# The opening of a hybrid attention layer: who loads the identity, the first norm's weights and x's first columns, and who casts the first weights

## The chip, the cores and the metric

The kernel runs on one core of one Trainium2 chip. The metric is the device time of one execution in microseconds (us); lower is better. A time given as a median is that of several runs; times inside an execution come from one profiled execution, counted from the start of its span.

## The reference, cut to what matters

One layer over 256 tokens of 2048 features, in float32. The change touches only how the layer begins: the first RMSNorm and the first columns of the first projection.

```python
def rms_norm(x, g):
    y = x32 * lax.rsqrt(jnp.mean(x32 * x32, axis=-1, keepdims=True) + EPS)
    return (y * g).astype(x.dtype)

h = rms_norm(x, attn_norm[layer])          # x is (1, 256, 2048)
proj = h @ w_in_l                          # (2048, 6152): q, k, v of two head groups, 8 forget gates
...                                        # forgetting attention and stick-breaking attention
x = x + merged @ w_out_l
x = x + conv_ffn(rms_norm(x, ffn_norm))    # two further products, a depthwise convolution of width 3
```

## The kernel before, in words

Tokens lie in 128 partitions, as two tiles `xt[0]` and `xt[1]` of 128 tokens (`x2`, line 82). For the projection x is needed with features in partitions, so TensorE (PE) transposes it: a 128x128 block of x times an identity matrix. `transposed_split(k, g)` (line 130) does this for the two blocks of columns k and k+1: four transposes into one PSUM tile `ps_x`, then two ScalarE (ACT) instructions that multiply by the norm's weight of each feature (`g`, one number for each partition) and round to fp32r, the high part of `hT` (line 140), then two VectorE (DVE) instructions that compute what the rounding left, the low part (line 143). The factor 1/rms of each token is applied later to the product's rows.

Weights are handled in the same way: a piece lands in a raw tile, one instruction casts it to fp32r (`w_hi`) and a DVE subtraction gives `w_lo`. Each product is three matmuls: high times high, low part of hT times high, high times low.

The norm's weights reach the kernel as 16 rows of 128 (`prow[:KT]`). `columns(ga, ...)` (line 123) turns them into 16 columns: one PE transpose with the identity (line 125) and one DVE copy (line 126). So the identity (`cs[:, :P]`, 64 KB of the constants) and `prow` come ahead of the first transposed x.

`opening()` (line 353) computes the first 512 columns of the projection in 8 chunks of 256 features. Its loads, casts and products are written out in order by hand: inside the block at line 429 a manual schedule keeps PE, DVE, ACT and SyncE (SP) in the order of the program, so an instruction that waits holds up all that stands behind it on its engine. GpSimd (POOL) is not in that list, and has no other work in the opening than to fill the tile `zeros`.

- `load_x(k, n)` (line 86) loads n blocks of columns of both token tiles, always by SP.
- `load_w(c, queue, which)` (line 359) loads chunk c of the weights, 256 rows of 512 columns. Chunk 0 is loaded as two halves of 128 rows, 256 KB each; below, the first half and the second half.
- `split_w(c)` (line 368) casts and subtracts. For the first half of chunk 0 it calls `transposed_split(0, ga)` between the cast and the subtraction (line 376).
- `multiply(c, i, n, high)` (line 381) issues the matmuls on a piece, first those with `w_hi`, then those with `w_lo`.
- `keep_busy(n)` (line 347) issues n matmuls of zeros whose result nobody reads, so that PE does not stand still. They need the tile `zeros` (line 343), which POOL fills.

The order of the issues and of the first work is lines 391 to 405:

```python
            load_x(0, 2)
            nc.sync.dma_start(cs[:, :P], cst[:, :P])
            load_w(0, nc.scalar, [0])
            nc.scalar.dma_start(prow[:KT, :], attn_norm[0].rearrange("(n p) -> n p", p=P))
            load_w(0, nc.scalar, [1])
            act.preload_act_table_set("natural_log_exp_and_others")
            load_x(2, 2)
            load_w(1)
            load_x(4, 4)
            load_w(2)
            keep_busy(17)
            columns(ga, prow[:KT, :], KT)
            keep_busy(0)
            split_w(0)
            keep_busy(6)
```

After this, `behind(c)` transposes the next two blocks of x and casts the next chunk while PE multiplies the present one. Raw weight tiles have three buffers (line 279), so the load of chunk 3 waits until chunk 0 has been subtracted. Everything after the opening (the rest of the projection, both attentions, the output projection, the feed-forward part from line 652 on) is the same in both kernels.

Of the kernel before, what the change touches and what calls it, by code (L numbers as in the profile page):

```python
# [14 lines left out]
P = 128  # L15
# [3 lines left out]
KT = D // P  # L19
# [22 lines left out]
def hybrid_layer(  # L42
# [19 lines left out]
    nc = tc.nc  # L62
    act, dve = nc.scalar, nc.vector
    xf = x.rearrange("b s d -> (b s) d")
# [9 lines left out]
    def f32(t):  # L74
        return t.bitcast(F32)
# [3 lines left out]
    cs = const.tile([P, C_MF], F32, name="cs")  # L79
    prow = const.tile([50, P], F32, name="prow")  # L80
    bf = const.tile([P, NH], F32, name="bf")
    x2 = big.tile([P, NT, D], F32, name="x2")
    xt = [x2[:, t, :] for t in range(NT)]
    xp = xf.rearrange("(t p) d -> p t d", p=P)

    def load_x(k, n):
        nc.sync.dma_start(x2[:, :, k * P : (k + n) * P], xp[:, :, k * P : (k + n) * P])
# [35 lines left out]
    def columns(dst, rows, n):  # L123
        pp = psb.tile([P, 512], F32, name="pp", tag="t")
        nc.tensor.transpose(pp[:, :n], rows, ident[:n, :n])
        dve.tensor_copy(dst, pp[:, :n])
# [3 lines left out]
    def transposed_split(k, g):  # L130

        ps = psb.tile([P, 2, S], F32, name="ps_x", tag="t")
        for j in range(2):
            for t in range(NT):
                nc.tensor.transpose(  # L135
                    ps[:, j, t * P : (t + 1) * P], xt[t][:, (k + j) * P : (k + j + 1) * P], ident
                )
        for j in range(2):
            i = k + j
            act.activation(hT[:, i, 0, :], ps[:, j, :], AF.Identity, scale=g[:, i : i + 1])  # L140
        for j in range(2):
            i = k + j
            dve.scalar_tensor_tensor(
                hT[:, i, 1, :], ps[:, j, :], g[:, i : i + 1], f32(hT[:, i, 0, :]),
                op0=ALU.mult, op1=ALU.subtract,
            )

    def sums_of_squares(ss, c, tiles=range(NT)):

        for t in tiles:  # L150
            junk = late.tile([P, 512], F32, name="junk", tag="raw", bufs=4)
            act.activation(junk, xt[t][:, c * 512 : (c + 1) * 512], AF.Square, accum_out=ss[:, t, c : c + 1])
# [55 lines left out]
    def rows_of(w, k0, n, c0, cols):  # L208
        return w[k0 * P : (k0 + n) * P, c0 : c0 + cols].rearrange("(k p) c -> p k c", p=P)
# [14 lines left out]
    def of_half(h, part, t):  # L224
        return h[:, part, t * P : (t + 1) * P]
# [48 lines left out]
    with ExitStack() as actx:  # L274
# [66 lines left out]


        zeros = at.tile([P, S], mybir.dt.bfloat16, name="zeros")
        nc.gpsimd.memset(zeros, 0.0)
        idle = pss.tile([P, S], F32, name="idle", tag="s")

        def keep_busy(n):
            for _ in range(n):
                nc.tensor.matmul(idle, zeros[:, :P], zeros, start=True, stop=True)
# [3 lines left out]
        def opening():  # L353

            acc = psa.tile([P, NT, 512], F32, name="acc", tag="acc")
            pairs = [[(0, 1), (1, 1)]] + [[(0, 2)]] * 7
            raws, parts = [], []

            def load_w(c, queue=nc.sync, which=(0, 1)):
                if c == len(raws):  # L360
                    raws.append(wraw.tile([P, 2048], F32, name="w_raw", tag="w_raw"))
                for i, n in pairs[c][which[0] : which[-1] + 1]:
                    queue.dma_start(
                        raws[c][:, i * 512 : (i + n) * 512].rearrange("p (a b) -> p a b", a=n),
                        rows_of(wi, 2 * c + i, n, 0, 512),
                    )

            def split_w(c):
                hi = whi.tile([P, 2048], F32R, name="w_hi", tag="w_hi")
                lo = wlo.tile([P, 2048], F32R, name="w_lo", tag="w_lo")  # L370
                parts.append([t[:, :1024].rearrange("p (a b) -> p a b", a=2) for t in (hi, lo)])
                for i, n in pairs[c]:
                    cols = slice(i * 512, (i + n) * 512)
                    act.copy(hi[:, cols], raws[c][:, cols])
                    if c == i == 0:
                        transposed_split(0, ga)
                    dve.tensor_tensor(
                        lo[:, cols], raws[c][:, cols], f32(hi[:, cols]), op=ALU.subtract
                    )

            def multiply(c, i, n, high):
                hi, lo = (p[:, i : i + n] for p in parts[c])
                order = [(j, l, hi) for j in range(n) for l in range(2)] if high else [(j, 0, lo) for j in range(n)]
                for m, (j, l, r) in enumerate(order):
                    for t in range(NT):
                        nc.tensor.matmul(  # L386
                            acc[:, t, :], of_half(hT[:, 2 * c + i + j], l, t), r[:, j, :],
                            start=high and c == i == m == 0, stop=not high and c == 7 and m == n - 1,
                        )

            load_x(0, 2)
            nc.sync.dma_start(cs[:, :P], cst[:, :P])
            load_w(0, nc.scalar, [0])
            nc.scalar.dma_start(prow[:KT, :], attn_norm[0].rearrange("(n p) -> n p", p=P))
            load_w(0, nc.scalar, [1])
            act.preload_act_table_set("natural_log_exp_and_others")
            load_x(2, 2)
            load_w(1)
            load_x(4, 4)
            load_w(2)  # L400
            keep_busy(17)
            columns(ga, prow[:KT, :], KT)
            keep_busy(0)
            split_w(0)
            keep_busy(6)

            def behind(c):
                transposed_split(2 * c + 2, ga)
                split_w(c + 1)

            for c in range(8):
                if 0 < c < 7:
                    behind(c)
                for i, n in pairs[c]:
                    if i == 0:
                        if c:
                            sums_of_squares(ss1, c // 2, [c % 2])
                        if c < 5:
                            if c % 2:
                                load_x(8 + 4 * (c // 2), 4)  # L420
                            load_w(c + 3)
                    for high in (True, False):
                        multiply(c, i, n, high)
                        if c == i == 0 and high:
                            behind(0)
                            sums_of_squares(ss1, 0, [0])
            return acc

        with tc.high_priority(offset=AHEAD), tc.manual_schedule(
            engines={mybir.EngineType.PE, mybir.EngineType.DVE, mybir.EngineType.Activation, mybir.EngineType.SP}  # L430
        ):
            acc_q0 = opening()
# [23 lines left out]
        for j in range(3):  # L456
            acc = project(2 * WF + 344 * j, 344)
            n = 344 if j < 2 else 336
# [546 lines left out]
```

## Time and profile before

| | |
|---|---|
| median of 3 runs | 1116.93 us (1116.54 to 1117.72) |
| the profiled execution's own time | 1115.63 us |
| its span, first to last instruction | 1113.7 us |
| granted TensorE clock, mean | 1.000 |
| PE busy | 1106.9 us, 99% of the span |
| DVE busy | 862.7 us, 77% |
| ACT busy | 692.7 us, 62% |
| POOL busy | 27.2 us, 2% |

The profiled execution is 1.93 us longer than its span, and 1.30 us under the median. In the views, PE stands for matmuls and transposes, PEld for the loading of their stationary operand, SPq, ACTq and POOLq for the issuing of transfers by SP, ACT and POOL. A row of the timeline gives start and duration in us, engine, source line, operation, output and inputs, the count of instructions merged into the row, and in square brackets how long the engine had been idle and what ended that. In the DMA view q1 is SP's queue, q10 is ACT's, q0 is POOL's; a window of this view counts the packets that moved in it, and their megabytes (millions of bytes). The view's KB are 1024 bytes.

### The profile page before, as it was taken

The numbers are of one execution on the slowest core, as the hardware profiler recorded it, in microseconds if no ns is written. First come the engines' busy times: TensorE is split into PE (matmuls) and PEld (weight loads), VectorE is DVE, ScalarE is ACT, GpSimd is POOL, SyncE is SP. The second block draws the span as 40 slices with busy tenths as digits, with TensorE's granted clock in tenths as the row PEclk, the third lists the DMA queues.
The fourth block names the chain that finished last, engine by engine and source line by source line (L and its number), as shares of the span: only waits on it lengthen the run. The fifth ranks groups of instructions, "written<-read, shape, count | busy, mean of one in ns | idle before, by whom it ended". The sixth has DMA issues, their size and how long they took to land.

```text
span 1113.7 us, 14715 instructions
## 1 busy us (share of the span) xinstructions
PE 1106.9 (99%) x5873; PEld 957.9 (86%) x5873; DVE 862.7 (77%) x906; ACT 692.7 (62%) x849; POOL 27.2 (2%) x27
## 2 busy tenths in 40 slices
PE   9999999999999999999999999999999999999998
PEld 7998888888888888888888888888888888888886
DVE  5745666657666677788899898989989899989973
ACT  6544545355565567666777767775777667776751
POOL 0000000000000000000000000000000000000000
PEclk9999999999999999999999999999999999999999
DMA  8676656564445486496869696788859697697941
GB/s 260 213 227 227 190 152 189 155 185 153 152 152 164 137 271 207 126 263 181 259 211 254 208 265 218 227 243 228 248 184 251 219 266 248 193 266 195 297 161 67
DMA packets 172479, 231.34 MB, mean 208 GB/s; under 512 B 4192, under 2 KB 118266, under 8 KB 172282
## 3 DMA queue, kind: packets, MB, share of 16 engines
q1 hardware_dynamic: 162378, 209.93, 58.3%
q0 software_dynamic: 9712, 19.93, 10.2%
q8 instruction: 46, 0.75, 0.3%
q10 hardware_dynamic: 320, 0.53, 0.2%
q14 instruction: 23, 0.19, 0.0%
HBM read 228.28 MB, written 2.11 MB: 207 GB/s over the span
## 4 chain that ended last, share of the span: by engine, by line
PE 98%; DVE 1%; DMA 0%; ACT 0%; issue 0%; SPq 0%; DVEq 0%; ACTq 0%
PE pu L246 33%; PE acc L219 24%; PE pu L253 18%; PE bank_a L219 10%; PE bank_b L219 4%; PE bank_c L219 2%; PE acc L386 2%; PE ps_x L135 1%; DVE w_lo L198 1%; DMA cs<-in_cst_dram 0%; PE ps_z L576 0%; PE ps_o L604 0%; PE ps_s L506 0%; PE ps_o L536 0%; PE ps_h L294 0%; PE ps_p L530 0%
## 5 line engine op out<-in xcount | busy, mean ns | idle before, releaser
L198 DVE TENSOR_TENSOR w_lo<-w_raw,w_hi 128x2048 fp32r<-128x2048 f32 (+2 forms) x200 | 440.1, 2204 | 161.9 <-ACT w_hi L197 156.0
L197 ACT CAST w_hi<-w_raw 128x2048 fp32r<-128x2048 f32 (+2 forms) x200 | 368.1, 1841 | 239.4 <-PE acc L219 91.2
L246 PE MATMUL pu<-hT,w_hi 128*128 128x512 f32 x1664 | 397.6, 391 | 0.0
L246 PEld LDWEIGHTS pu<-hT,w_hi 128*128 128x128 f32 x1664 | 310.1, 188 | 63.2
L253 PEld LDWEIGHTS pu<-hT,w_lo 128*128 128x128 f32 x1664 | 213.6, 191 | 8.2
L253 PE MATMUL pu<-hT,w_lo 128*128 128x256 f32 x1664 | 216.2, 283 | 0.0
L219 PE MATMUL acc<-w_hi,hT 128*128 128x512 f32 (+1 forms) x576 | 126.0, 370 | 0.0
L219 PEld LDWEIGHTS acc<-w_hi,hT 128*128 128x128 f32 x576 | 101.6, 188 | 14.3
L709 ACT ACTIVATE tap<-up,ccol 128x256 f32<-128x256 f32 x176 | 74.6, 495 | 0.0
L198 DVE TENSOR_TENSOR w_lo<-w_sum,w_hi 128x2048 fp32r<-128x2048 f32 (+1 forms) x30 | 62.2, 2073 | 13.4 <-ACT w_hi L197 10.6
L197 ACT CAST w_hi<-w_sum 128x2048 fp32r<-128x2048 f32 (+1 forms) x30 | 51.9, 1731 | 22.8 <-PE pu L246 22.8
L219 PE MATMUL acc<-w_lo,hT 128*128 128x512 f32 (+1 forms) x288 | 64.6, 366 | 0.0
L219 PEld LDWEIGHTS acc<-w_lo,hT 128*128 128x128 f32 x288 | 51.6, 188 | 7.5
L219 PE MATMUL acc<-w_hi,oT 128*128 128x512 f32 x192 | 46.3, 393 | 0.0
L219 PE MATMUL bank_a<-w_hi,g 128*128 128x512 f32 x176 | 44.2, 392 | 0.0
L219 PEld LDWEIGHTS acc<-w_hi,oT 128*128 128x128 f32 x192 | 35.4, 188 | 7.0
L219 PEld LDWEIGHTS bank_a<-w_hi,g 128*128 128x128 f32 x176 | 31.8, 189 | 5.7
L219 PE MATMUL bank_a<-w_hi,s 128*128 128x512 f32 x144 | 36.5, 393 | 0.0
L219 PE MATMUL bank_b<-w_hi,s 128*128 128x512 f32 x144 | 36.4, 392 | 0.0
L714 DVE TENSOR_TENSOR gate<-gate,tap 128x512 f32<-128x512 f32 x44 | 30.3, 688 | 2.3
L714 DVE TENSOR_TENSOR val<-val,tap 128x512 f32<-128x512 f32 x44 | 30.3, 688 | 2.3
L815 POOL DMA_DIRECT2D w_raw<-in_w_down_dram x10 | 12.7, 1270 | 779.6 <-DVE s L761 373.9
(176 smaller groups left out, 1052.1 us busy)
## 6 DMA issues: line engine op xcount, KB each, us to landing
w_raw<-in_w_up_dram SPq DMA_DIRECT2D x88, 1024.0 KB, 5.8
w_raw<-in_w_down_dram SPq DMA_DIRECT2D x40, 1024.0 KB, 5.3
w_raw<-in_w_in_dram SPq DMA_DIRECT2D x36, 1024.0 KB, 5.3
w_raw<-in_w_out_dram SPq DMA_DIRECT2D x16, 1024.0 KB, 5.2
w_raw<-in_w_in_dram SPq DMA_DIRECT2D x12, 688.0 KB, 4.2
w_raw<-in_w_down_dram POOLq DMA_DIRECT2D x8, 1024.0 KB, 12.0
w_sum<-in_w_down_dram POOLq DMA_DIRECT2D x8, 1024.0 KB, 9.0
w_raw<-in_w_down_dram SPq DMA_DIRECT2D x8, 512.0 KB, 4.0
```

The source lines that it names most:

```text
L135: nc.tensor.transpose(ps[:, j, t * P : (t + 1) * P], xt[t][:, (k + j) * P : (k + j + 1) * P], ident)
L197: act.copy(hi[:, :n], raw[:, :n])
L198: dve.tensor_tensor(lo[:, :n], raw[:, :n], f32(hi[:, :n]), op=ALU.subtract)
L219: nc.tensor.matmul(o, lhs(i, l, t), r[:, i, :], start=starts and j == 0, stop=stops and j == 3 * n - 1, skip_group_check=more,)
L246: nc.tensor.matmul(acc[:, j, :], hi[:, i, j * P : (j + 1) * P], hT[:, k].rearrange("p a b -> p (a b)"), start=k == 0, stop=False,)
L253: nc.tensor.matmul(acc[:, j, S:], lo[:, i, j * P : (j + 1) * P], hT[:, k, 0, :], start=False, stop=k == KT - 1,)
L386: nc.tensor.matmul(acc[:, t, :], of_half(hT[:, 2 * c + i + j], l, t), r[:, j, :], start=high and c == i == m == 0, stop=not high and c == ...
L709: act.activation(taps[w][:, j, :], u[:, j, w : w + S], AF.Copy, scale=ccol[:, w, f : f + 1])
L714: dve.tensor_tensor(a, a, tap, op=ALU.add)
L815: nc.gpsimd.dma_start(mem[into][:, : nk * 512].rearrange("p (a b) -> p a b", a=nk), src, accum_op=ALU.add)
```

## The change

The tile of zeros is filled by DVE and no longer by POOL. The identity and the 16 rows of the norm's weights are loaded by POOL's queue, and no longer by SP's and ACT's. The first two blocks of x's columns come as two transfers of 128 KB: tokens 0 to 127 by SP, tokens 128 to 255 by ACT, each as that queue's first. The first half of chunk 0 follows on SP, the second half on ACT (before, both were on ACT, with the norm's weights between them). The cast of the first half is done by DVE, the second half's still by ACT. Two of the 23 matmuls of zeros go: 17 become 16, and 6 become 5.

```diff
         zeros = at.tile([P, S], mybir.dt.bfloat16, name="zeros")
-        nc.gpsimd.memset(zeros, 0.0)
+        dve.memset(zeros, 0.0)
...
                 for i, n in pairs[c]:
                     cols = slice(i * 512, (i + n) * 512)
-                    act.copy(hi[:, cols], raws[c][:, cols])
                     if c == i == 0:
+                        dve.tensor_copy(hi[:, cols], raws[c][:, cols])
                         transposed_split(0, ga)
+                    else:
+                        act.copy(hi[:, cols], raws[c][:, cols])
                     dve.tensor_tensor(
                         lo[:, cols], raws[c][:, cols], f32(hi[:, cols]), op=ALU.subtract
                     )
...
-            load_x(0, 2)
-            nc.sync.dma_start(cs[:, :P], cst[:, :P])
-            load_w(0, nc.scalar, [0])
-            nc.scalar.dma_start(prow[:KT, :], attn_norm[0].rearrange("(n p) -> n p", p=P))
+            nc.gpsimd.dma_start(cs[:, :P], cst[:, :P])
+            nc.gpsimd.dma_start(prow[:KT, :], attn_norm[0].rearrange("(n p) -> n p", p=P))
+            for t, queue in enumerate((nc.sync, nc.scalar)):
+                queue.dma_start(xt[t][:, : 2 * P], xf[t * P : (t + 1) * P, : 2 * P])
+            load_w(0, nc.sync, [0])
             load_w(0, nc.scalar, [1])
             act.preload_act_table_set("natural_log_exp_and_others")
             load_x(2, 2)
             load_w(1)
             load_x(4, 4)
             load_w(2)
-            keep_busy(17)
+            keep_busy(16)
             columns(ga, prow[:KT, :], KT)
-            keep_busy(0)
             split_w(0)
-            keep_busy(6)
+            keep_busy(5)
```

## The prediction, as put on record before the result was known

> **What bounds the kernel now.** I read the page first: busy time, then the chain that ended last.
>
> ```profile
> span 1113.7 us, 14715 instructions
> PE 1106.9 (99%) x5873; PEld 957.9 (86%) x5873; DVE 862.7 (77%) x906; ACT 692.7 (62%) x849; POOL 27.2 (2%) x27
> PE 98%; DVE 1%; DMA 0%; ACT 0%; issue 0%; SPq 0%; DVEq 0%; ACTq 0%
> ```
>
> PE is on the chain for 98%. Nothing in the change takes work from it, so it can only move the moment from which PE works without holes. The chain of waits in the first 31 us shows where that moment comes from:
>
> ```profile
> 1.23 4.08 DMA cs<-in_cst_dram
> 5.45 0.20 PE pp L125
> 5.65 0.60 PE ps_x L135 x4
> 6.28 0.85 ACT hT L140 x2
> 7.15 0.49 DVE hT L143
> 10.79 0.44 PE ps_x L135 x4
> 14.01 0.44 PE ps_x L135 x4
> ```
>
> Until 5.45 us the chain is the landing of the identity; from then on work, and from 10.79 a chunk every 3.22 us. I call 5.45 **T**: the start of the transpose at line 125, behind which every transposed x waits. The forecast is how far T moves, as long as what follows keeps its distance from T. The timeline shows what stands around T:
>
> ```profile
> 0.74 0.45 ACTq L363 DMA_DIRECT2D w_raw<-in_w_in_dram  x1
> 0.74 0.44 SPq L87 DMA_DIRECT2D x<-in_x_dram  x1
> 1.10 3.34 PE L349 MATMUL idle<-zeros 128*128 128x256 bf16 x17 [1.10 <-POOL zeros L344]
> 1.22 0.49 ACTq L394 DMA_DIRECT2D prow<-in_attn_norm_dram  x1
> 1.74 0.43 SPq L87 DMA_DIRECT2D x<-in_x_dram  x1
> 2.21 0.47 SPq L363 DMA_DIRECT2D w_raw<-in_w_in_dram  x1
> 4.74 0.62 ACT L374 CAST w_hi<-w_raw 128x512 fp32r<-128x512 f32 x1 [1.24 <-DMA w_raw<-in_w_in_dram]
> 5.42 0.13 PEld L125 LDWEIGHTS pp<-cs,prow 16*128 16x128 f32 x1 [1.25 <-DMA prow<-in_attn_norm_dram]
> 5.97 0.64 PEld L349 LDWEIGHTS <-zeros 128*128 128x128 bf16 x6
> 6.80 0.30 PEld L386 LDWEIGHTS acc<-w_hi,hT 128*128 128x128 f32 x2 [0.19 <-ACT hT L140]
> ```
>
> PE stands still for 1.0 us between the zeros (to 4.44) and T. The identity and the norm's weights (prow) both end that wait; the first weights, cast at 4.74, don't.
>
> **When bytes move.** The DMA view in windows from 0 to 3.6, 4.3, 5.0, 5.8, 7.2 and 8.5 us:
>
> ```profile
> DMA packets 237, 0.33 MB, mean 92 GB/s; under 512 B 0, under 2 KB 152, under 8 KB 237
> DMA packets 512, 0.58 MB, mean 135 GB/s; under 512 B 39, under 2 KB 382, under 8 KB 512
> DMA packets 787, 0.84 MB, mean 168 GB/s; under 512 B 64, under 2 KB 617, under 8 KB 787
> DMA packets 968, 1.10 MB, mean 190 GB/s; under 512 B 74, under 2 KB 712, under 8 KB 968
> DMA packets 1227, 1.57 MB, mean 217 GB/s; under 512 B 99, under 2 KB 755, under 8 KB 1227
> DMA packets 1497, 2.09 MB, mean 245 GB/s; under 512 B 115, under 2 KB 771, under 8 KB 1497
> ```
>
> This is a clock made of bytes: a transfer is through when everything ahead of it has moved. x's first columns (256 KB), the identity (64 KB) and prow (8 KB) are 0.336 MB; before, the first weight half (0.262 MB) moves among them. I also need the time from last packet to a start. The window from 0 to 4.7 has 64 packets under 512 B, 16 for each of the first four transfers, as I read them; T follows 0.75 us later:
>
> ```profile
> DMA packets 702, 0.73 MB, mean 154 GB/s; under 512 B 64, under 2 KB 560, under 8 KB 702
> ```
>
> I take 0.7 us as that lag.
>
> **The change, part by part.**
>
> *POOL's queue.* The trace has no load of this kind by POOL. The nearest row is its small transfer at 92.53 us, and beside it one at 638.33 into a busy queue; the q0 row between the first two is the window 93.7 to 94.1, and the last two are q1 in 638.4 to 642.2 and q0 in 642.2 to 644:
>
> ```profile
> 92.53 0.69 POOL L492 DMA_DIRECT2D c_rows<-mine  x1 [91.49 <-ACT mine L491]
> q0 software_dynamic: 32, 0.01, 10.6%
> 94.61 0.59 POOL L493 DMA_DIRECT2D minus_c<-c_rows  x1 [1.39 <-DMA c_rows<-mine]
> 637.82 0.37 SPq L190 DMA_DIRECT2D w_raw<-in_w_down_dram  x1
> 638.33 1.28 POOL L815 DMA_DIRECT2D w_raw<-in_w_down_dram  x1 [40.41 <-ACT tap L709]
> q1 hardware_dynamic: 498, 0.94, 85.9%
> q0 software_dynamic: 101, 0.21, 71.8%
> ```
>
> With idle DMA engines, packets move some 1.2 us after POOL's start and whoever waits goes on 2.1 us after it (94.61). Into a queue that SP had filled half a microsecond earlier, nothing of POOL's moves for 3.9 us, until SP's transfer has moved. So POOL's delay lies between 1.2 us and that plus all that is ahead. Now place the two. The identity starts at 0.74 (POOL's memset stood there) and moves from about 2.0, among x's halves: first packets of SP's and ACT's first transfers are in 1.8 to 1.9 and in 2.2 to 2.3,
>
> ```profile
> q1 hardware_dynamic: 6, 0.01, 23.6%
> q10 hardware_dynamic: 3, 0.01, 54.1%
> ```
>
> so SP needs 1.1 us from issue to first packet and ACT 1.5. Prow starts behind the identity, 0.74 + 0.69 = 1.43, and is ready at about 2.7. The weight halves, issued at 1.23, are ready at 2.3 (SP) and 2.7 (ACT). **Prow, the smallest transfer, is the one that comes last.** With nothing of the weights ahead (0.336 MB) it has moved by 3.6 and T is 4.3; behind the first half (0.6 MB) 4.35 and 5.05; behind both (0.86 MB) 5.05 and 5.75. I take T = 4.85, behind most of the first half, since that one is ready 0.4 us before prow and the other isn't: **-0.6 us**; ends of the term -1.15 and +0.3.
>
> *x on two queues, the weights behind.* Bytes decide, not queues: x now moves without the weights among it, and is through with the identity or before. The first half (SP, in the slot of the identity) and the second (ACT, 1.22 and no longer 1.74) are both through at 0.86 MB, 5.05, and land at about 5.7. SP's number of issues is the same, so x's next columns and chunk 1 stay at 1.74 and 2.21; the table load moves up by 0.5 us in ACT's idle time. Nothing.
>
> *The cast by DVE.* The trace has no copy of 128x512 on DVE from SBUF. The nearest are a one-input instruction of half the width and a two-input one of the same:
>
> ```profile
> L525 DVE TENSOR_SCALAR pr<-pr,rl 128x256 f32<-128x256 f32 x8 | 2.8, 347 | 0.0
> L377 DVE TENSOR_TENSOR w_lo<-w_raw,w_hi 128x512 fp32r<-128x512 f32 x2 | 1.3, 680 | 0.0
> ```
>
> The bounds are 0.35 and 0.68 us; I take 0.5, in the middle. It waits for the first half (5.7), so it ends at 6.2. PE needs it with the first hT, 1.35 us behind T (6.80 - 5.45): at 6.2. Behind it on DVE stand the low parts of hT, due 1.70 behind T (7.15 - 5.45), at 6.55, and PE waits for those. So it is just hidden: nothing. With T at 4.3 the cast would end 0.2 us after those are due (6.0), and that much is lost. On ACT the cast filled a gap before hT; its removal gives nothing.
>
> *Zeros by DVE.* POOL's memset took 0.31 us; DVE takes between nothing and that, and PE starts at 0.8 to 1.1. Its zeros, 0.2 us each, end by 4.3 and not at 4.44; the wait for T covers this. It is also the floor: T can't come before 4.2. The sixth of the later zeros (0.1 us) lies in PE's wait for ACT (0.19 idle at 6.80): nothing.
>
> *What is late next.* Chunk 1 is through at 1.65 MB (7.4), lands at 8.1, and is cast at 9.62 now; x's columns 4 to 7 are through at 2.17 MB (8.7), land at 9.4, and PE transposes them at 10.40:
>
> ```profile
> 9.62 1.05 ACT L374 CAST w_hi<-w_raw 128x1024 fp32r<-128x1024 f32 x1
> 10.40 0.59 PEld L135 LDWEIGHTS ps_x<-cs,x 128*128 128x128 f32 x4
> ```
>
> Moved up by 0.6 both still have their data; the second has 0.4 us left, which caps the gain at about 1.0.
>
> **The sum.** Profiled execution 1115.63 (span 1113.7 and 1.93 around it): -0.6 gives 1115.0. The median shown is 1.30 above that execution; from it, 1116.93 - 0.6 = **1116.3 us**. That is 0.05%. A measurement of this kernel can tell about 0.2% (2.2 us) from no change.
>
> **The rivals.**
>
> *Queues take turns.* If the DMA engines take a packet from each queue in turn, prow passes the weights: T = 4.3, and with the cap of x's columns the gain is 1.0: **1115.9**. For: SP's and ACT's packets do mix in the opening. Against: the row at 638.33, where POOL's waited for all of SP's. [...]
>
> *Behind both halves, or x's next columns too.* Slower POOL, or ACT as quick as SP: T = 5.75, +0.3, **1117.2**; with x's columns 2 and 3 ahead (issued 1.74; 1.12 MB, 5.85, T 6.55) +1.1, **1118.0**.
>
> *Slower: prow behind chunk 1.* SP issues chunk 1 at 2.21, ready at 3.3. If POOL's two first transfers take 0.6 us more than the row at 92.53 (1.28 us for each, as at 638.33, would do), prow comes in behind 1.65 MB: 7.4, T = 8.1, +2.65: **1119.6**. The point from which it decides: prow ready after 3.3 and served in order of arrival. For: 638.33. Against: the 1.28 us are for transfers of 512 KB and more that add; those of lines 492 and 493 took 0.6 to 0.7.
>
> *The clock.* The first 17 zeros run at 0.2 us each (3.34 in all), the later six at 0.1 (0.64): PE starts at half pace. If a longer hole before T brought that back, chunk 0 would run at half pace: 12 matmuls by some 0.2 us, +2.5, **1118.8**. Against: the present hole of 1.0 us cost nothing.
>
> **How the numbers follow.** Forecast 0.45 (1116.2 to 1116.5); queues take turns 0.25; behind both halves or the next columns 0.17; behind chunk 1 0.10; clock 0.03. The runs shown scatter from 0.4 below to 0.8 above their median. The range 1115.5 to 1118.0 takes in the first three cases, 0.87, less what scatter carries out. Slower by over 0.2% (above 1119.2) is chunk 1's case and a little of the clock's: 0.11. Faster by over 0.2% would need T before 3.3, under the floor of the zeros: 0.03 for what I don't see. The rest, 0.86, is within.
>
> **What the profile after would show.** T, the start of line 125 and what ended the wait: prow rather than the identity, at 4.7 to 5.1. Prow's issue by POOL at about 1.4. A DVE cast of about 0.5 us that ends by 6.2. The first PEld at line 386 at T + 1.35, and the second chunk's pace of 3.2 us. Wrong would be: T over 5.4, a hole at line 386 that waits for the cast, or at line 135 for x.

## The result, and the profile after

The changed kernel takes **1118.8 us** (median of 22 runs, 1117.34 to 1120.06). The kernel before takes 1115.78 (22 runs beside them, 1115.16 to 1117.72). The ratio is **1.0025, with a 95% interval from 1.0019 to 1.0031**: slower by 3.0 us, where the forecast was 0.6 us faster. The base is 1.15 us below the median of the three runs that the prediction started from, so it is the difference that is compared in what follows. The profiled execution took 1120.06 us (before 1115.63); it is the slowest of the 22.

The page after:

```profile
span 1117.9 us, 14712 instructions
PE 1108.8 (99%) x5871; PEld 959.0 (86%) x5871; DVE 863.0 (77%) x908; ACT 691.8 (62%) x848; POOL 27.7 (2%) x28
```

PE runs two instructions fewer and is busy 1.9 us longer (1106.9 before): besides a later start, some of its work has become slower. The chain of waits says where (start, duration, what):

```profile
1.28 0.70 POOL cs L393
1.99 4.85 DMA prow<-in_attn_norm_dram
...
6.97 0.20 PE pp L125
...
8.32 2.11 PE acc L388 x4
10.43 0.85 PE ps_x L135 x4
...
13.60 0.44 PE ps_x L135 x4
...
16.79 0.44 PE ps_x L135 x4
```

Three things are to be seen. T, the start of line 125, is 6.97 and not 5.45: +1.52. What ended the wait is prow, as foretold, but it was issued at 1.99 and landed at 6.84 (1.99 + 4.85). And PE's rows after T are too long: four transposes take 0.85 us where they take 0.44 from 13.60 on, and the four matmuls ahead of them 2.11. When the steady pace of a chunk in 3.19 us is reached (13.60 to 16.79; before 10.79 to 14.01), the kernel is 2.8 us behind: 1.5 from T, and 1.3 that were lost between T and 13.60. The distance stays at that until far behind the opening: SP's load at 637.82 in the kernel before starts at 640.56 here. The profiled execution then loses 1.3 us more in the feed-forward part, most of it in one wait:

```profile
668.80 2.06 PE L219 MATMUL bank_a<-w_hi,s 128*128 128x512 f32 x8 [1.06 <-DVE x L794]
```

In the kernel before the same matmuls (664.85) wait for nothing. So this span is 4.2 us longer, more than the medians differ. Whether the change has a part in this late wait was not tried; what follows is about the 2.8 us of the opening.

The timeline has the reason for the first part:

```profile
0.74 0.39 SPq L396 DMA_DIRECT2D x<-in_x_dram  x1
0.83 0.17 DVE L344 MEMSET zeros<- 128x128 uint32 x1 [0.83 <-PEq L992]
1.06 3.60 PE L349 MATMUL idle<-zeros 128*128 128x256 bf16 x16 [1.06 <-DVE zeros L344]
1.18 0.45 ACTq L363 DMA_DIRECT2D w_raw<-in_w_in_dram  x1
1.19 0.42 SPq L363 DMA_DIRECT2D w_raw<-in_w_in_dram  x1
1.28 0.71 POOL L393 DMA_DIRECT2D cs<-in_cst_dram  x1 [0.84 <-POOLq L992]
1.65 0.43 SPq L87 DMA_DIRECT2D x<-in_x_dram  x1
1.99 0.55 POOL L394 DMA_DIRECT2D prow<-in_attn_norm_dram  x1
2.12 0.47 SPq L363 DMA_DIRECT2D w_raw<-in_w_in_dram  x1
6.97 0.20 PE L125 MATMUL pp<-cs,prow 16*128 16x16 f32 x1 [2.31 <-DMA prow<-in_attn_norm_dram]
7.30 0.42 DVE L375 CAST w_hi<-w_raw 128x512 fp32r<-128x512 f32 x1
8.32 0.30 PEld L388 LDWEIGHTS acc<-w_hi,hT 128*128 128x128 f32 x2 [0.30 <-ACT hT L140]
```

POOL's first transfer starts at 1.28, not at 0.74 where its memset used to stand. By then both weight halves are issued (1.18, 1.19); when prow follows at 1.99, x's columns 2 and 3 are too (1.65). So prow comes behind the identity and 1.05 MB of x and weights that were issued before it. PE has used up its zeros at 4.66 and stands still for 2.31 us (the bracket at 6.97), not 1.0. The windows by whole microseconds show what that costs; the column after the busy times is the granted clock, then DMA share and GB/s:

```profile
8.00:9.00 1.00, 0.98 (x5) 0.32 (x3) 0.33 (x1) 1.00 (x3) 0.00 (x0) 0.87 1.06 404
9.00:10.00 1.00, 1.00 (x3) 0.70 (x3) 1.00 (x3) 0.14 (x1) 0.00 (x0) 0.50 0.85 319
...
12.00:13.00 1.00, 1.00 (x6) 0.82 (x5) 0.81 (x2) 1.00 (x3) 0.00 (x0) 0.93 0.70 188
```

A clock of 0.87 in the first window is full for 0.74 of it and half for 0.26, so the half clock begins at 8.74; 0.93 in the last ends it at 12.14. For **3.4 us PE runs at half speed** in this execution, and such a stretch does 1.7 us less work than a full one.

### The profile page after: what moved, and what is told of

Its sections match the earlier page's. It is cut to its first block, busy times and chain, and to the rows that moved or that the text cites. A ratio compares the mean times of both kernels' runs of the same rounds, so it can differ in the third digit from the quotient of the medians.

```text
span 1117.9 us, 14712 instructions
## 1 busy us (share of the span) xinstructions
PE 1108.8 (99%) x5871; PEld 959.0 (86%) x5871; DVE 863.0 (77%) x908; ACT 691.8 (62%) x848; POOL 27.7 (2%) x28
## 3 DMA queue, kind: packets, MB, share of 16 engines
HBM read 228.28 MB, written 2.11 MB: 206 GB/s over the span
## 4 chain that ended last, share of the span: by engine, by line
PE 97%; DVE 1%; DMA 0%; ACT 0%; issue 0%; POOL 0%; DVEq 0%; ACTq 0%; POOLq 0%
PE pu L246 33%; PE acc L219 24%; PE pu L253 17%; PE bank_a L219 10%; PE bank_b L219 4%; PE bank_c L219 2%; PE acc L388 2%; PE ps_x L135 1%; DVE w_lo L198 1%; DMA prow<-in_attn_norm_dram 0%; ACT w_hi L197 0%; PE ps_z L578 0%; PE ps_s L508 0%; PE ps_o L606 0%; PE ps_o L538 0%; PE ps_h L294 0%
```

## The experiments

**Theory.** Prow is served in order of arrival, behind all that was ready before it; POOL is ready late; the longer hole then costs the clock besides. **Rivals**: POOL's queue is slow in itself, or slow for 16 short rows, whatever stands ahead; or the loss comes from the other parts of the change, the cast by DVE or the fewer zeros. For each kernel I give T against the 5.45 of before, the shift of the steady pace (chain, against 10.79 or 14.01) and the median against that of before's runs beside it (1115.74, 1115.72 and 1115.95).

| kernel | T | steady pace | median us | ratio (95%) |
|---|---|---|---|---|
| the change | +1.52 | +2.8 | 1118.80, +3.0 | 1.0025 (1.0019 to 1.0031) |
| more zeros | +1.41 | +1.4 | 1117.07, +1.3 | 1.0009 (1.0000 to 1.0018) |
| prow by ACT | +0.08 | +1.4 | 1116.84, +1.1 | 1.0008 (1.0000 to 1.0017) |
| POOL's part alone | +2.75 | +3.5 | 1119.35, +3.6 | 1.0032 (1.0020 to 1.0045) |
| without POOL | -1.09 | +1.6 | 1116.26, +0.5 | 1.0004 (0.9995 to 1.0013) |
| nothing ahead of POOL | -1.00 | +1.6 | 1116.76, +1.0 (one run) | |
| before, with the hole | -0.19 | +1.2 | 1117.14, +1.4 | 1.0008 (1.0000 to 1.0017) |
| cast alone | -0.26 | -0.3 | 1116.85, +1.1 | 1.0007 (0.9998 to 1.0016) |
| identity and prow first | -0.61 | +1.3 | 1116.43, +0.7 | 1.0005 (0.9996 to 1.0014) |
| two queues, weights apart | +0.64 | +0.95 | 1116.13, +0.2 | 1.0001 (0.9992 to 1.0010) |
| prow before the identity | +1.48 | +2.1 | 1118.15, +2.2 (one run) | |

T and the pace are of one execution, the median is of many, so they needn't agree to better than about 1 us (see the kernel without POOL). Nor does a median alone show a loss of 1 us: of the 27 runs of the kernel before that stand beside "cast alone", 17 took 1115.13 to 1115.85 us and ten 1116.56 to 1117.90, with a mean clock of 0.999 or 1.000 in both groups. What parts them was not found. The intervals of more zeros, prow by ACT and before with the hole only just reach down to no change.

**POOL's part alone**: the kernel before, with the identity and prow on POOL and the zeros by DVE (POOL had to be free for that); x, weights and cast as before.

```diff
-        nc.gpsimd.memset(zeros, 0.0)
+        dve.memset(zeros, 0.0)
...
-            nc.sync.dma_start(cs[:, :P], cst[:, :P])
+            nc.gpsimd.dma_start(cs[:, :P], cst[:, :P])
...
-            nc.scalar.dma_start(prow[:KT, :], attn_norm[0].rearrange("(n p) -> n p", p=P))
+            nc.gpsimd.dma_start(prow[:KT, :], attn_norm[0].rearrange("(n p) -> n p", p=P))
```

> The kernel before with only the identity and the norm's weights moved to POOL's queue, and the zeros filled by DVE; x in one transfer by SP, both halves of chunk 0 by ACT, the cast by ACT. Theory, the move to POOL is the whole loss: T at 6.5 to 7.1 us, half clock after it in most executions, 2.3 to 3.0 us above the kernel before. Rival, the split of x or the cast by DVE costs: within 0.5 us of the kernel before.

One row of its timeline and two of its chain:

```profile
1.74 0.46 SPq L363 DMA_DIRECT2D w_raw<-in_w_in_dram  x1
```

```profile
1.98 6.09 DMA prow<-in_attn_norm_dram
...
14.32 0.44 PE ps_x L135 x4
```

It is the worst kernel of all, and worse than expected, so this part alone more than accounts for the loss. Prow landed 1.2 us later than in the changed kernel, though POOL issued it at the same moment. What differs is SP: here it had one issue fewer ahead and issued chunk 1 at 1.74, not at 2.12, which by order of arrival puts up to 0.5 MB more in front of prow (1.2 us at the 372 GB/s that this kernel moves from 6 to 7 us are 0.45 MB). T is 8.20; the prediction's slower rival had worked out 8.1 for prow behind chunk 1.

**Nothing ahead of POOL**: the changed kernel, with weights and x's later columns (up to chunk 2) moved from SP and ACT to POOL's queue, behind prow (`load_x` takes the queue as a third argument).

```diff
-            load_w(0, nc.sync, [0])
-            load_w(0, nc.scalar, [1])
+            load_w(0, nc.gpsimd, [0])
+            load_w(0, nc.gpsimd, [1])
...
-            load_x(2, 2)
-            load_w(1)
-            load_x(4, 4)
-            load_w(2)
+            load_x(2, 2, nc.gpsimd)
+            load_w(1, nc.gpsimd)
+            load_x(4, 4, nc.gpsimd)
+            load_w(2, nc.gpsimd)
```

> The changed kernel with every further load of the opening up to chunk 2 (both halves of chunk 0, x's columns 2 to 7, chunks 1 and 2) on POOL's queue behind the norm's weights, so that SP and ACT have only x's two halves under way when the norm's weights are ready. Only T counts here; the whole will be slower, since the weights come later. Theory, order of arrival (in the changed kernel prow, issued at 1.99 us, waits for what SP and ACT had sent off before): its packets move at about 3.2 us, T follows at 4.0 and with the zeros in the way at 4.7. Rival, POOL's first transfers are slow by themselves, 4.9 us from issue to landing as in the changed kernel: T at 6.8 to 7.0.

The list of issues in the DMA view (last column: us from issue to landing), first of the changed kernel, then of this one:

```profile
cs<-in_cst_dram POOLq DMA_DIRECT2D x1, 64.0 KB, 4.6
prow<-in_attn_norm_dram POOLq DMA_DIRECT2D x1, 8.0 KB, 4.8
```

```profile
cs<-in_cst_dram POOLq DMA_DIRECT2D x1, 64.0 KB, 2.9
prow<-in_attn_norm_dram POOLq DMA_DIRECT2D x1, 8.0 KB, 2.3
```

The same two transfers, by the same queue, at the same times (prow 1.97 and 1.99), take 1.7 and 2.5 us less when only x's first columns and a few small loads are ahead. So the queue isn't slow in itself. The 2.5 us come with what stood in front. Had the DMA engines taken turns so short that a small transfer gets by, prow would have passed the weights in the changed kernel also; in that form, the prediction's, the rival "queues take turns" falls with this pair. The pair doesn't refute longer turns: turns as long as a whole transfer would have put prow in about the same place. Against turns of that length speaks POOL's part alone. There the first transfers of SP and ACT are 0.52 MB, and 0.54 MB had moved by 4.3 us; from 4.3 to 5.0 us SP's queue moved 0.14 MB more and ACT's 0.07 MB, of their second transfers, and POOL's had moved nothing by 5.0, though its identity had been issued at 1.27. So order of arrival is what fits the kernels with loads by POOL, without being measured directly. The kernel gains nothing from its T of 4.45, since x's later columns now come late by POOL (columns 4 to 7 land at 12.06).

Its trace shows something else, which the account of the clock needs: PE waits 1.80 us for x's columns 2 and 3, and the granted clock (1.00 behind the busy times) stays full in every window from 7 to 13 us.

```profile
9.42 0.66 PE L135 MATMUL ps_x<-cs,x 128*128 128x128 f32 x4 [1.80 <-DMA x<-in_x_dram]
```

```profile
8.00:9.00 1.00, 0.00 (x0) 0.00 (x0) 0.37 (x1) 0.00 (x0) 0.00 (x0) 1.00 0.93 332
```

**Prow before the identity**: the two lines of POOL's loads swapped.

```diff
-            nc.gpsimd.dma_start(cs[:, :P], cst[:, :P])
             nc.gpsimd.dma_start(prow[:KT, :], attn_norm[0].rearrange("(n p) -> n p", p=P))
+            nc.gpsimd.dma_start(cs[:, :P], cst[:, :P])
```

> The changed kernel with POOL's two loads in the other order: the norm's weights at 1.3 us, the identity behind them at 1.8. Theory, what counts is when a transfer is ready on POOL's queue and not which it is: now the identity is the one behind the two halves of chunk 0 and x's next columns, and T stays at 6.3 to 7.0 us. Rival, it is the 16 short rows of the norm's weights that are slow by POOL: T at 5.4 to 5.8, as in the run with the identity alone on POOL.

Two rows of its timeline and one of its chain:

```profile
1.28 0.67 POOL L393 DMA_DIRECT2D prow<-in_attn_norm_dram  x1 [0.84 <-POOLq L992]
1.94 0.61 POOL L394 DMA_DIRECT2D cs<-in_cst_dram  x1
```

```profile
1.94 4.85 DMA cs<-in_cst_dram
```

Whichever is second takes 4.85 us. It is the place in the order, not the 16 short rows.

**More zeros**: the changed kernel with 28 zeros ahead of T, which shortens the hole and touches no transfer.

```diff
-            keep_busy(16)
+            keep_busy(28)
```

> The changed kernel with 28 matmuls of zeros ahead of line 125 instead of 16, so that PE has work until the norm's weights are there. T (start of line 125) stays at 7.0 us. Theory, a loss in two parts (T later by 1.5 us, and a hole of 2.3 us before T after which PE's clock is granted at half for 3.4 us, 1.3 us more): the half clock goes, the first chunk runs at full pace, and of the 3.0 us lost 1.5 remain: 1.5 us (0.14%) above the kernel before. Rival, late data or the cast by DVE slow the first chunk: nothing changes, 2.7 to 3.0 us (0.26%) above the kernel before.

From its timeline, and from its windows:

```profile
1.06 4.78 PE L349 MATMUL idle<-zeros 128*128 128x256 bf16 x28 [1.06 <-DVE zeros L344]
6.86 0.20 PE L125 MATMUL pp<-cs,prow 16*128 16x16 f32 x1 [1.02 <-DMA prow<-in_attn_norm_dram]
```

```profile
9.00:10.00 1.00, 0.90 (x6) 0.77 (x6) 1.00 (x4) 0.03 (x1) 0.00 (x0) 1.00 0.95 357
```

T is nearly as late as in the changed kernel (6.86), the hole is 1.02 us, the clock stays full, and **1.7 of the 3.0 us are gone** (1118.80 to 1117.07; before was 1115.78 and 1115.74 beside them). What is left, +1.3, is T's +1.4. So the loss has two parts, and the zeros tell them apart: 1.3 us for the late prow and 1.7 for the clock. All 11 runs lie between 1116.92 and 1117.29, the narrowest of all these kernels; not one of the changed kernel's 22 (from 1117.34) is as fast.

The clock is paid for in two ways. One is the half clock from 8.74 to 12.14. But of the changed kernel's 22 runs the seven with a mean clock of 0.997 or 0.998 have a median of 1118.83, and the fifteen with 0.999 or 1.000 one of 1118.80. The other way is seen with prow before the identity, which has the same T: there PE is still at half pace behind T.

```profile
7.11 1.11 PE L135 MATMUL ps_x<-cs,x 128*128 128x128 f32 x4
```

In the changed kernel's trace the same four take 0.65 us. Half pace from the start on is not counted in the mean clock (1.000 in the run with that row). Which way each of the other runs went, no trace shows.

**Before, with the hole**: the kernel before with fewer zeros ahead of T.

```diff
-            keep_busy(17)
+            keep_busy(6)
```

> The kernel before with 6 matmuls of zeros ahead of line 125 instead of 17 and nothing else: a hole of about 3 us before T, while T stays at 5.45 us and all transfers are as before. Theory, the hole itself sets PE's clock to half for one or two stretches of 3.4 us: chunk 0 and part of the next run at half pace, 1.3 to 3 us above the kernel before. Rival, the clock follows something else (the late data, the queues): within 0.3 us of the kernel before.

From its timeline and its chain:

```profile
1.10 1.46 PE L349 MATMUL idle<-zeros 128*128 128x256 bf16 x6 [1.10 <-POOL zeros L344]
```

```profile
5.52 1.04 PE ps_x L135 x4
...
7.84 1.71 PE acc L386 x4
9.55 0.56 PE ps_x L135 x4
...
11.97 0.44 PE ps_x L135 x4
```

No transfer is changed and T is even 0.2 earlier (5.26), but the kernel is 1.4 us slower by its median. Transposes take 1.04 us for four (0.60 before, 0.44 later), and the first four matmuls 1.71: PE is still at half pace until the transposes of 9.55. So a hole costs clock without POOL, and without a later T.

**Prow by ACT**: the changed kernel with prow on ACT's queue behind x; the identity alone stays with POOL.

```diff
-            nc.gpsimd.dma_start(prow[:KT, :], attn_norm[0].rearrange("(n p) -> n p", p=P))
             for t, queue in enumerate((nc.sync, nc.scalar)):
                 queue.dma_start(xt[t][:, : 2 * P], xf[t * P : (t + 1) * P, : 2 * P])
+            nc.scalar.dma_start(prow[:KT, :], attn_norm[0].rearrange("(n p) -> n p", p=P))
```

> The changed kernel with the norm's weights back on ACT's queue, behind x's second half and ahead of the second half of chunk 0; the identity stays with POOL. Theory, prow comes last because POOL issues it second and it then stands behind 0.8 MB of the other queues: now the identity ends the wait, whose packets moved until 5.1 us in the changed kernel, so T at 5.6 to 5.9, a hole of 1.1 us that keeps the clock, and 0.2 to 0.5 us above the kernel before. Rival, POOL's queue costs the same for whatever it carries: T stays near 7.0 and the loss near 3 us.

From its timeline and its chain:

```profile
1.06 3.59 PE L349 MATMUL idle<-zeros 128*128 128x256 bf16 x16 [1.06 <-DVE zeros L344]
5.53 0.28 PE L125 MATMUL pp<-cs,prow 16*128 16x16 f32 x1 [0.88 <-DMA cs<-in_cst_dram]
```

```profile
1.27 4.21 DMA cs<-in_cst_dram
...
5.82 1.05 PE ps_x L135 x4
```

T is 5.53, just under what was expected: POOL's first transfer, ready about 0.7 us sooner than the second, lands 1.4 us sooner (1.27 + 4.21 = 5.48, against prow's 6.84). The time is higher than expected. In this execution PE has not reached full pace at T, behind a hole of 0.88 us: four transposes take 1.05 us. I had left the clock out of this expectation.

**Without POOL**: the changed kernel, with the identity by SP and prow by ACT, each behind x's half and ahead of the weights.

```diff
-            nc.gpsimd.dma_start(cs[:, :P], cst[:, :P])
-            nc.gpsimd.dma_start(prow[:KT, :], attn_norm[0].rearrange("(n p) -> n p", p=P))
...
+            nc.sync.dma_start(cs[:, :P], cst[:, :P])
+            nc.scalar.dma_start(prow[:KT, :], attn_norm[0].rearrange("(n p) -> n p", p=P))
             load_w(0, nc.sync, [0])
```

> The changed kernel with the identity on SP's queue (behind x's first half, ahead of the first half of chunk 0) and the norm's weights on ACT's (behind x's second half); the split of x, the cast by DVE and the zeros by DVE stay. Theory, bytes ahead decide: x, identity and norm's weights are the first 0.336 MB, T at 4.4 to 4.8 us, not before the zeros end (4.66), no hole, and 0.6 to 1.0 us (0.07%) below the kernel before. Rival, x's split or the cast on DVE costs something of its own: T is early but the first chunk's pace is reached no earlier, within 0.3 us of the kernel before or above.

Its timeline, its windows, and the DMA view from 3.6 to 5.6 us:

```profile
4.36 0.20 PE L125 MATMUL pp<-cs,prow 16*128 16x16 f32 x1
6.77 0.43 DVE L375 CAST w_hi<-w_raw 128x512 fp32r<-128x512 f32 x1 [2.00 <-DMA w_raw<-in_w_in_dram]
7.34 2.04 PE L388 MATMUL acc<-w_hi,hT 128*128 128x512 f32 x4 [1.65 <-DVE w_hi L375]
```

```profile
7.00:8.00 1.00, 0.66 (x2) 0.59 (x3) 1.00 (x4) 0.58 (x1) 0.00 (x0) 0.66 1.02 386
10.00:11.00 1.00, 1.00 (x5) 0.86 (x4) 0.00 (x0) 0.72 (x2) 0.00 (x0) 0.64 0.90 270
```

```profile
DMA packets 261, 0.45 MB, mean 224 GB/s; under 512 B 24, under 2 KB 61, under 8 KB 261
```

T is 4.36, at the zeros' floor, and nothing comes of it: the first weights, cast at 6.77, are late next. In these two microseconds the DMA engines move 224 GB/s. The same view of the kernel before:

```profile
DMA packets 690, 0.72 MB, mean 360 GB/s; under 512 B 68, under 2 KB 537, under 8 KB 690
```

Why the rate falls is open. PE waits 1.65 us for the cast, and the half clock returns from 7.32 (0.66) to 10.72 (0.64), again 3.4 us. The runs part by this: eight with a mean clock of 0.999 or 1.000 took 1115.76 to 1116.41, three with 0.998 took 1117.30 to 1117.69. In this kernel the runs whose mean shows the half clock are some 1.4 us slower, three against eight. The expected gain of T wasn't there even in the first eight (0.0 to 0.7 above before's median).

**Two queues, weights apart**: no load by POOL; SP takes x's half and the identity, ACT x's half, the first weights, then prow; 21 zeros, cast by DVE.

```diff
-            nc.gpsimd.dma_start(cs[:, :P], cst[:, :P])
-            nc.gpsimd.dma_start(prow[:KT, :], attn_norm[0].rearrange("(n p) -> n p", p=P))
...
-            load_w(0, nc.sync, [0])
+            nc.sync.dma_start(cs[:, :P], cst[:, :P])
+            load_w(0, nc.scalar, [0])
+            nc.scalar.dma_start(prow[:KT, :], attn_norm[0].rearrange("(n p) -> n p", p=P))
...
-            keep_busy(16)
+            keep_busy(21)
```

> A try for a version better than both: the changed kernel with nothing on POOL's queue. SP issues x's first half, then the identity; ACT x's second half, the first half of chunk 0, the norm's weights, the second half; 21 matmuls of zeros so that PE has no hole before T; the cast by DVE stays. Theory, order of arrival and the hole: what T needs and the first half of chunk 0 are together 0.6 MB, T at 4.9 to 5.2 us, the weights in time for DVE's cast, no half clock: 0 to 0.5 us below the kernel before, which a measurement can't tell from it. Rival, the weights issued 0.45 us later are late as in the run without POOL before: T early, a hole at line 388, 0.3 to 1.5 us above.

Prow, ACT's third issue, landed at 5.96 and T was 6.09, later than expected. No half clock returned, but in spite of the 21 zeros PE was still at half pace at T (the transposes at 6.35 take 0.85 us, 0.44 later). The time can't be told from before's.

**Identity and prow first**: the kernel before, with SP's identity ahead of x and ACT's prow ahead of the weights.

```diff
-            load_x(0, 2)
             nc.sync.dma_start(cs[:, :P], cst[:, :P])
-            load_w(0, nc.scalar, [0])
+            load_x(0, 2)
             nc.scalar.dma_start(prow[:KT, :], attn_norm[0].rearrange("(n p) -> n p", p=P))
+            load_w(0, nc.scalar, [0])
```

> The kernel before with the order on each queue turned round: SP issues the identity ahead of x's first columns, ACT the norm's weights ahead of the first half of chunk 0; nothing goes to POOL, x stays one transfer, the cast stays on ACT. A try for a version better than both. Theory, order of arrival: the two small ones pass at once, x is through with 0.6 MB at 4.4 us where the identity was at 4.65, T at 5.1 to 5.3, 0.2 to 0.4 us (0.03%) below the kernel before, less than can be measured. Rival, later weights take it back: the first half, issued 0.45 us later, is cast after hT is due, and the time is up to 0.5 us above.

Line 125 ran at 4.84, but x landed at 5.83, later than expected, and its transposes began at 5.88, at half pace (1.12 us for four). What was put last here came last; the sum of the bytes is the same.

**Cast alone**: the kernel before, with only the zeros' memset and the first cast moved to DVE.

```diff
-        nc.gpsimd.memset(zeros, 0.0)
+        dve.memset(zeros, 0.0)
...
-                    act.copy(hi[:, cols], raws[c][:, cols])
                     if c == i == 0:
+                        dve.tensor_copy(hi[:, cols], raws[c][:, cols])
                         transposed_split(0, ga)
+                    else:
+                        act.copy(hi[:, cols], raws[c][:, cols])
```

> The kernel before with only the zeros filled and the first half of chunk 0 cast by DVE; all loads as before, 17 and 6 matmuls of zeros. Theory, these two edits are hidden: DVE's cast starts behind the copy of the norm's columns, takes 0.42 us as in the changed kernel, and ends 0.4 us before PE needs it; T at 5.4 us, within 0.3 us of the kernel before. Rival, the cast delays the low parts of hT behind it on DVE: up to 0.5 us above.

```profile
5.53 0.42 DVE L375 CAST w_hi<-w_raw 128x512 fp32r<-128x512 f32 x1
6.54 0.30 PEld L388 LDWEIGHTS acc<-w_hi,hT 128*128 128x128 f32 x2 [0.19 <-ACT hT L140]
```

With T at 5.19 in its trace, the first weights are loaded 1.35 us behind T, exactly as in the kernel before, and the wait there is still ACT's hT. In the trace the cast costs nothing. The median doesn't settle it: the runs lie in two groups, five from 1115.65 to 1116.17 and six from 1116.85 to 1117.32, much as those of the kernel before beside it do, and the interval includes no change.

No kernel here beats the one before.

## Why the prediction was wrong, point by point

**"The identity starts at 0.74 (POOL's memset stood there) ... Prow starts behind the identity, 0.74 + 0.69 = 1.43, and is ready at about 2.7": this step failed.** The duration was right (0.71 measured against 0.69), the start was not. In all six kernels with loads by POOL, the first began at 1.26 to 1.28, and the second, in the five that have one, at 1.94 to 1.99. With the 1.2 us of the row at 92.53, prow is ready at 3.2, not 2.7. Half a microsecond matters because SP's next issues fall into it.

**The byte clock held to within half a microsecond for the loads by POOL, and order of arrival fits them.** With "ready at 3.2" the prediction's own working gives the rival "x's next columns too" (T 6.55, +1.1) and stops just short of "behind chunk 1", whose point was "prow ready after 3.3". Measured are 6.97 for the first, and 8.20 against 8.1 where SP issued chunk 1 earlier. The changed kernel sits between the two, at the edge that the prediction named, and the forecast was placed a whole rival too early: T was forecast 0.6 us earlier and came 1.5 later. Where POOL loads nothing the byte clock was worse: x's transposes began at 5.88 for an expected T of 5.1 to 5.3 (identity and prow first), and T was 6.09 for 4.9 to 5.2 (two queues).

**The clock was taken for a rival of its own, with 0.03: the second failure.** Its condition, a longer hole, was no separate accident. It follows from each of the rivals with a later T, which held 0.27 together, and each of them should have carried a share of its price. "The present hole of 1.0 us cost nothing" is true and was a weak argument against: holes of 1.65 us (without POOL) and 2.31 came with a half clock. One of 1.80 (nothing ahead of POOL) did not, so length alone doesn't decide it, and what does is open. The size was put at 2.5 us (12 matmuls by 0.2); more zeros measure 1.7, which is what one stretch of 3.4 us at half speed can lose.

**The sum by the runs** is +1.3 (T, what more zeros leave) + 1.7 (clock, what more zeros take away) = +3.0. The two add up by construction, being differences of three medians; what checks them is the traces, where more zeros leave T 1.4 us late and a stretch at half speed can lose 1.7. The forecast was -0.6 + 0. Behind x's columns with the clock, the prediction's own prices would have given +1.1 + 2.5 = +3.6.

**Queues take turns** had 0.25 and falls, in the form that lets prow pass the weights, as the rows of 638 us had said.

**Right**: the zeros by DVE cost nothing (0.17 us, PE starts at 1.06, before at 1.10) and set a floor (T 4.36 and 4.45 where the loads were early). The cast was put at 0.5 us, measured 0.42, and is hidden: the first weights are loaded at T + 1.35 (8.32). A chunk takes 3.2 us again. That x on two queues would help nothing agrees with the two kernels without POOL, neither of which can be told from before.

**"What is late next"** named chunk 1 and x's columns 4 to 7 as the cap on an earlier T, and took the first weights to be there at 5.7. Without POOL the first weights landed at 6.74, at 224 GB/s. It did not matter for the change, whose T was late, but even a right forecast of T = 4.4 would have promised a gain that isn't there.

## What to carry to other kernels

Here an 8 KB load that everything waits for took 4.8 us from issue to landing behind the identity and 1.05 MB issued before it, and 2.3 us with only the identity, x's first columns and a few small loads ahead: its place counted, not its size. So write down when each queue's issue is *ready*, with the engine's real first issue, and count the bytes of all queues ahead of it. Before a later start is priced, look at what PE does meanwhile: a hole that lengthens can cost a stretch at half clock besides (here 3.4 us, which do 1.7 us less work), so the two are one case and one sum. If the wait can't be avoided, fill the hole; twelve matmuls of zeros won back 1.7 of 3.0 us.

## What the runs showed of the hardware that was not expected

- **POOL's first transfer** began at 1.26 to 1.28 us in six kernels, while its memset began at 0.73 to 0.74 in those where POOL filled the zeros, and SP's and ACT's first transfers at 0.73 to 0.74. What holds it was not tried.
- **The half clock lasted 3.4 us** in each of the three traces whose clock column shows it in the opening: 8.74 to 12.14 in the changed kernel, 7.32 to 10.72 without POOL, 7.94 to 11.34 in POOL's part alone (0.97 in the window from 7 to 8 us, 0.83 from 11 to 12). The holes near its start were of 2.31, 1.65 and 3.44 us. A hole of 1.0 us (before; more zeros) did not bring the half clock, and neither did one of 1.80 (nothing ahead of POOL). So the length of a hole is not shown to be the rule. From the start, when PE is still at half pace, a hole of 0.88 us came with a longer stay there (prow by ACT: four transposes at 5.82 take 1.05 us, those at 5.65 in the kernel before 0.60).
- **When PE first reaches full pace differs from trace to trace.** PE's zeros start at 1.05 to 1.10 us in all of them, but the trace's own clock entries begin, with full clock, at 3.83 us (before) and 5.32 (the change), and four transposes still take 1.04 us at 5.52 (before with the hole) and at 7.18 (prow before the identity). Whether this is why one program has runs 1.4 us apart (without POOL) was not tried. The clock column reads 1.00 until the first change on record, also while PE is at half pace from the start (1.04 us for four transposes in the kernel before with the hole); there only the durations tell.
- **224 GB/s** from 3.6 to 5.6 us, where the kernel before moves 360, when the weights came behind the identity and prow (without POOL): not explained. Prow by ACT has it too (231 GB/s, the mean of its five windows of 0.4 us in that time); the changed kernel moves 344.
